# Loading the feed-forward weights of a two-layer diffusion trunk: split on chip from one copy, or by a casting and an accumulating DMA

## The chip, the cores and the metric

The kernel runs on one core of a Trainium2 chip. The metric is the device time of one execution in microseconds (us), as the median of several executions. TensorE (PE) multiplies, VectorE (DVE), ScalarE (ACT) and GpSimd (POOL) work on elements, SyncE (SP) issues DMAs; POOL can issue DMAs too.

## The reference, cut to what matters

Two layers, a mixer and a gated ConvFFN in each, over 640 tokens (512 latent, 128 context) of 1024 features, all in float32:

```
def conv_ffn(h, w_up, w_conv, w_down):
    a, g = jnp.split(h @ w_up, 2, axis=-1)
    return (jax.nn.gelu(dwconv3(a, w_conv)) * g) @ w_down
```

`w_up` has 2 x 2816 output features and `w_down` maps 2816 features back to 1024. The result must be as good as float32, so the kernel writes every operand of a large product as a sum of a high part in the reduced float32r format and a low part, the rest, and adds three products: high x high, high x low and low x high.

## The kernel before, in words

Features lie on partitions, tokens on columns. A *block* is one weight tile of 128 input rows x 8 (or 7) k-tiles x 128 outputs: 128 partitions x 1024 (or 896) float32 values, 512 KB (or 448 KB). For a block PE runs, in `mm_k` (L118), 3 products x 2 halves of 320 tokens for each k-tile: 48 matmuls, or 42 where there are 7 k-tiles. They add up in a pair of PSUM banks; there are two such pairs (L1213 and L1089: `use_psum(2, 4)`).

The feed-forward layer `ffn` (L373) has 22 feature groups f. Each takes an *up* block for `a` and one for `g`. After the `a` block, ACT and DVE convolve it out of PSUM (`conv3`, L350 and L353) and ACT takes the GELU (L388); after the `g` block, DVE multiplies (L398), and ACT and DVE split the product G into its parts (L400, L401). The *down* product runs in three passes (GROUPS, L29: k-tiles 0 to 8, 8 to 15, 15 to 22), each after the up blocks that it needs, 8 blocks a pass. So a layer has 44 up and 24 down blocks. The first three up blocks run together (`head=3`) while the norm before them is still being finished.

Weights come through `load_w` (L101): SP loads a raw block into one of 4 buffers, ACT casts it into the high part (L97), and an engine subtracts to get the low part (L98). That engine is POOL for the blocks of a head and DVE for all others. High and low parts have 3 buffers each:

```
wh = wp.tile([P, 1024], F32R, tag="wh", name=f"{nm}h")
wl = wp.tile([P, 1024], F32R, tag="wl", name=f"{nm}l")
act.copy(out=wh[:, :n], in_=raw[:, :n])
eng.tensor_tensor(out=wl[:, :n], in0=raw[:, :n], in1=wh[:, :n].bitcast(F32), op=ALU.subtract)
```

In layer 0, DVE also works on the conditioning of the other sub-layers beside the feed-forward blocks: 56 tiles `adw` of 512 KB, each loaded by SP (L244) and used by two reductions (L247).

A scheduler writes the instruction order of each engine from the program; every engine then executes its own list in order and waits at its head. A DMA waits on the issuing engine's queue, and what stands behind it waits too.

Of the kernel before, what the change touches and what calls it, by code (L numbers as in the profile page):

```python
# [10 lines left out]
F32 = mybir.dt.float32  # L11
F32R = mybir.dt.float32r
AF = mybir.ActivationFunctionType
# [3 lines left out]
P = 128  # L17
# [19 lines left out]
def trunk(ctx: ExitStack, tc: tile.TileContext, I, O, dbg=None, stop=None):  # L37
# [4 lines left out]
    wp = ctx.enter_context(tc.tile_pool(name="wp", bufs=3))  # L42
    psum = {}

    def use_psum(pairs, singles):
        """the 8 banks of PSUM: so many tiles of two banks and of one"""
        if "es" in psum:
            psum["es"].close()
        es = psum["es"] = ExitStack()
        psum["shape"] = pairs, singles  # L50
        n = psum["n"] = psum.get("n", 0) + 1
        kw = dict(space=bass.MemoryType.PSUM, reuse_waits="tile")
        psum["m"] = es.enter_context(tc.tile_pool(name=f"pm{n}", bufs=pairs, **kw))
        psum["s"] = es.enter_context(tc.tile_pool(name=f"ps{n}", bufs=singles, **kw))
# [7 lines left out]
    def bank(pt, a):  # L62
        """half a of a tile of two banks, or of two tiles of one"""
        return pt[a] if isinstance(pt, tuple) else pt[:, a]

    # ---------------------------------------------------------------- constants and persistent data
# [21 lines left out]
    # ---------------------------------------------------------------- weights: load, exact split  # L88
    def load_raw(src, nm):
        raw = wp.tile([P, 1024], F32, tag="raw", name=nm, bufs=4)  # L90
        sp.dma_start(out=raw, in_=src)
        return raw
# [7 lines left out]

    def load_w(src, nm, nk=KT, eng=dve):  # L101
        raw = wp.tile([P, 1024], F32, tag="raw", name=nm, bufs=4)
        sp.dma_start(out=raw[:, : nk * P], in_=src)
        wh, wl = split_w(raw, nk * P, nm, eng)
        return wh.rearrange("p (k c) -> p k c", c=P), wl.rearrange("p (k c) -> p k c", c=P)
# [19 lines left out]
    def linear(srcs, done, nm, ks=None, nk=KT, head=2, tail=0, by_half=True, split=SPLIT, filler=None,  # L125
               kcut=None, pre=(), hook=None, spare=False, pooled=(), x_last=False):
        """ks: (k index in the weight tile, xh, xl) in the order of arrival; head: so many first tiles run with
        k outermost; tail: so many last ones finish half by half; spare: the tile after the head in single banks;
        x_last: in the head, the low parts of the tokens come after those of the weights"""
# [4 lines left out]
        while i < n:  # L134
            left = n - i
            g = min(head, left) if i == 0 and head else (tail if tail and left == tail else 1)
            # while a norm holds the vector engine
            eng = pool if i == 0 and head and by_half or i in pooled else dve
# [40 lines left out]
    # tokens on partitions: out[tile] = X[:, tile]^T W, W 512 columns wide  # L179
# [17 lines left out]
    # ---------------------------------------------------------------- adaLN modulation  # L197
# [10 lines left out]
    # on the tensor engine, two blocks (chunk, half of it) of 512 features at once; in four steps  # L208
# [29 lines left out]
    # on the vector engine: rows of W^T times the conditioning vectors; list of steps, one per 128 features  # L238
# [17 lines left out]
    # ---------------------------------------------------------------- RMSNorm (+ adaLN), by halves of the tokens  # L256
    # (start, end, request group) of each half, and overlapping windows of 128 tokens that cover it
# [6 lines left out]
    def rms_steps(nm, a, nrm):  # L264
        """1/rms of the tokens of half a, in every partition of a PSUM tile; in two steps"""
# [18 lines left out]
        # one Newton step of 1/sqrt  # L284
# [26 lines left out]
    def norm_steps(l, which, nrm):  # L311
        """both halves, in seven steps for the end of the product before it"""
        n = 2 * l + which
        s0, s1 = (rms_steps(f"n{n}{a}", a, nrm) for a in range(2))
        next(s0)
        for _ in range(3):
            yield
        rb = next(s0)
        yield
        norm_part(l, which, nrm, 0, rb, range(0, 6))  # L320
        yield
        next(s1)
        rb1 = next(s1)
        norm_part(l, which, nrm, 0, rb, range(6, KT))
        yield
        yield norm_part(l, which, nrm, 1, rb1, range(KT))
# [8 lines left out]

    # ---------------------------------------------------------------- depthwise conv of width 3 along tokens
    # buffers: a column of padding, 512 latent tokens, padding, 128 context tokens, padding
    def halves(pt):
        """both halves of PSUM: the columns that are latent in both, and those latent in the first only"""
        return pt[:, :, 0 : NS - HT], pt[:, :, NS - HT : HT]  # L340

    def conv_parts(buf, d):
        """the same columns of a buffer, moved by d"""
        e = 1 if d > 1 else 0
        return (buf[:, 0 : 2 * HT].rearrange("p (a b) -> p a b", a=2)[:, :, d : d + NS - HT],
                buf[:, e : e + 2 * HT + 2].rearrange("p (a b) -> p a b", a=2)[:, :, NS - HT + d - e : HT + d - e])
# [9 lines left out]
    def tokens(buf):  # L356
        """(slice of the tokens, their columns of a buffer)"""
        return (slice(0, NS), buf[:, 1 : NS + 1]), (slice(P0, T), buf[:, NS + 2 : T + 2])
# [13 lines left out]
    # ---------------------------------------------------------------- ConvFFN  # L372
    def ffn(l, after, hook=None):  # L373
        with ExitStack() as es:
# [43 lines left out]
            def up(i0, i1):  # L418
                linear([I["w_up"][l, i // 2, i % 2] for i in range(i0, i1)], lambda i, pt, a: done_up(i0 + i, pt, a),
                       f"u{l}_{i0}_", head=3 if i0 == 0 else 0, filler=filler, spare=i0 == 0)  # L420

            nxt = 0
            for gi, (k0, k1) in enumerate(GROUPS):
                end = 2 * min(k1 + 1, NF)
                if end > nxt:
                    up(nxt, end)
                    nxt = end
                linear([I["w_down"][l, o, :, k0:k1] for o in range(KT)],
                       lambda o, pt, a: here.__setitem__(0, residual(l, 5, o, pt, a)), f"d{l}_{gi}_",
                       ks=[(k - k0, G[k][:, 0], G[k][:, 1]) for k in range(k0, k1)], nk=k1 - k0, head=0, filler=filler,  # L430
                       tail=3 if k1 == NF else 0, hook=hook)

    # ---------------------------------------------------------------- hyena filters (no data from x)
    def hyena_filters(fl, spectra):
        """in three parts: the loads, the filters, their spectra"""
# [18 lines left out]
        # the decay, where the first of the products with it will be  # L454
# [5 lines left out]
        for j, w in enumerate((w1, w2)):  # L460
# [18 lines left out]
            if j == 0:  # L479
                # sum and difference of the two filters' weights, twice (64 rows each), and their exact split  # L480
# [5 lines left out]
        # high parts of the hidden layer, then low parts  # L486
# [6 lines left out]
        for r in range(5):  # L493
# [8 lines left out]
            if r in (0, 4):  # L502
                # the filter of the future has no tap at 0: half of sum plus difference
# [34 lines left out]
    # ---------------------------------------------------------------- mixers A and B  # L538
    def mixer_ab():
        with ExitStack() as es:  # L540
# [9 lines left out]
            # weight tiles: (v, x1) x 4, x2 x 4, gates, q x 4, k x 4, o x 4  # L550
# [73 lines left out]
            # x holds u, then the convolved u (tiles 0-3), and x2, then y of the hyena (tiles 4-7)  # L624
            def hyena_chunk(j):
# [42 lines left out]
                # context sequence  # L668
# [64 lines left out]
            # running maxima: high parts from rows 0 and 32, low parts 64 rows further; and columns that pick both  # L733
# [7 lines left out]
            def mlstm_gates(pt, rows):  # L741
# [24 lines left out]
                # log_sigmoid(f) = min(f, 0) - log(u) + ((u - 1) - e), u = fl(1 + e)  # L766
# [79 lines left out]
            def head_a(h):  # L846
                q, k = qk[:, h], qk[:, 4 + h]
                # latent sequence
# [33 lines left out]
                # context sequence  # L882
# [19 lines left out]
            def head_b(h):  # L902
# [25 lines left out]
                # norm per head: rstd = exp(-ln(v)/2) and one Newton step  # L928
# [53 lines left out]
    # ---------------------------------------------------------------- mixer C  # L982
    # latent tokens of keys, values and queries go column by column of the grid: token c * 8 + r
    def mixer_c():
        with ExitStack() as es:
# [6 lines left out]
            # context keys of a head, the other head's rows zero  # L992
            kc = [[at.tile([P, P], F32, name=f"kc{b}{e}") for e in range(2)] for b in range(2)]
            # latent keys between 64 columns of padding, the high part twice and the low part once: with the queries
            # as (high, low) they give all products but low times low
            k1 = [[at.tile([P, 640], F32R, name=f"k1{b}{e}") for e in range(2)] for b in range(2)]
            k2 = [[at.tile([P, 640], F32R, name=f"k2{b}{e}") for e in range(2)] for b in range(2)]
            # 64 columns of padding, 512 latent tokens, 64 columns of padding, 128 context tokens
# [13 lines left out]
            # PSUM (rows 0-4 | rows 5-7, context) to column order  # L1012
# [300 lines left out]
def pack(i):  # L1313
# [10 lines left out]
    # (chunk, k pair, half, p, par, 512) and, for the other chunks, transposed (chunk, tile, p, 1024)  # L1324
# [44 lines left out]
    # rpbw[8 b + r, h, 8 a + r2]: bias of query (row r, column c) and key (row r2, column c + a - b - 8)  # L1369
# [45 lines left out]
```

## Time and profile before

| what | value |
|---|---|
| median of 3 runs | 1732.03 us (1731.26 to 1732.91) |
| profiled execution, span | 1733.2 us |
| PE busy | 1676.1 us, 97% |
| DVE busy | 1052.3 us, 61% |
| ACT busy | 672.4 us, 39% |
| POOL busy | 142.2 us, 8% |
| read from HBM | 169.61 MB |

The page gives the profiled execution by its span alone; it is 1.2 us above the median. Busy time is summed over the whole span, and the stages differ: the rows below are read by stage. The feed-forward layers lie at about 400 to 850 us and 1240 to 1710 us of the span. "Us to landing" of a DMA counts from its issue to the arrival of its last byte.

### The profile page before, as it was taken

The numbers are of one execution on the slowest core, as the hardware profiler recorded it, in microseconds if no ns is written. First come the engines' busy times: TensorE is split into PE (matmuls) and PEld (weight loads), VectorE is DVE, ScalarE is ACT, GpSimd is POOL, SyncE is SP. The second block draws the span as 40 slices with busy tenths as digits, with TensorE's granted clock in tenths as the row PEclk, the third lists the DMA queues.
The fourth block names the chain that finished last, engine by engine and source line by source line (L and its number), as shares of the span: only waits on it lengthen the run. The fifth ranks groups of instructions, "written<-read, shape, count | busy, mean of one in ns | idle before, by whom it ended". The sixth has DMA issues, their size and how long they took to land. (4 is left out here: it accounts for less than half of the span.)

```text
span 1733.2 us, 28191 instructions
## 1 busy us (share of the span) xinstructions
PE 1676.1 (97%) x11434; PEld 1596.5 (92%) x11434; DVE 1052.3 (61%) x2089; ACT 672.4 (39%) x1235; POOL 142.2 (8%) x150
## 2 busy tenths in 40 slices
PE   5999999999999999999997999999999999999997
PEld 2699889899999999999997888998999999999997
DVE  5886656666987677777376555555564433433444
ACT  6323346754432133223245565555343312321332
POOL 3110001101000000000023212120100000000001
PEclk9999999999999999999999999999999999999998
DMA  8334422141454454453213111211222222222211
GB/s 325 117 132 163 160 72 71 48 142 59 140 176 147 146 153 144 154 170 104 79 64 101 60 60 47 65 42 52 74 73 74 73 74 73 71 76 85 69 54 61
DMA packets 57121, 175.62 MB, mean 101 GB/s; under 512 B 7632, under 2 KB 15104, under 8 KB 56736
## 3 DMA queue, kind: packets, MB, share of 16 engines
q1 hardware_dynamic: 56800, 173.66, 31.1%
q8 instruction: 90, 1.47, 0.4%
q14 instruction: 39, 0.32, 0.1%
q0 software_dynamic: 192, 0.17, 0.0%
HBM read 169.61 MB, written 4.20 MB: 100 GB/s over the span
## 5 line engine op out<-in xcount | busy, mean ns | idle before, releaser
L331 DVE SCALAR_TENSOR_TENSOR x<-pd,mod,x 128x320 f32<-128x320 f32 (+2 forms) x144 | 55.1, 434 | 146.7 <-PE pd L122 137.3
L247 DVE CUSTOM_DVE_ANT_0 adj<-adw,cb 128x1024 f32<-128x1024 f32 x112 | 136.7, 1221 | 1.6
L398 DVE TENSOR_TENSOR pr<-pu,ge 128x384 f32<-128x384 f32 x84 | 37.4, 486 | 108.4 <-PE pu L122 107.6
L353 DVE SCALAR_TENSOR_TENSOR fcb<-pu,cwf,fcb 128x384 f32<-128x384 f32 (+1 forms) x176 | 95.8, 549 | 4.1
L388 ACT ACTIVATE ge<-fcb 128x641 f32<-128x641 f32 x44 | 32.6, 742 | 105.4 <-DVE fcb L353 105.4
L306 ACT ACTIVATE XH<-nt,mod 128x192 fp32r<-128x192 f32 (+1 forms) x96 | 39.6, 466 | 44.0 <-DVE nt L302 43.8
L1120 DVE CUSTOM_DVE_ANT_0 s<-pS,bm 128x384 f32<-128x384 f32 x64 | 34.5, 553 | 30.1 <-PE pS L1119 29.0
L307 DVE SCALAR_TENSOR_TENSOR XL<-nt,mod,XH 128x192 fp32r<-128x192 f32 (+1 forms) x96 | 46.4, 521 | 5.0 <-ACT XH L306 4.9
L1021 DVE TENSOR_SCALAR s<-s,nm 128x384 f32<-128x384 f32 (+1 forms) x80 | 46.3, 586 | 1.8
L1019 ACT ACTIVATE s<-s,nm 128x384 f32<-128x384 f32 x64 | 39.2, 612 | 20.3 <-DVE nm L1120 18.3
L350 ACT ACTIVATE fcb<-pu,cwf 128x384 f32<-128x384 f32 x88 | 46.3, 528 | 1.3
L1194 POOL TENSOR_TENSOR fo<-fo,rs 128x320 f32<-128x320 f32 x8 | 6.9, 888 | 469.8 <-ACT rs L1186 469.8
L1134 ACT COPY pTs<-pS 128x384 f32<-128x384 f32 (+1 forms) x80 | 33.7, 434 | 23.4 <-PE pS L1132 22.7
L1132 PE MATMUL pS<-ident,s 128*128 128x128 f32 x208 | 36.3, 281 | 5.8 <-DVE s L1021 5.8
L98 POOL TENSOR_TENSOR qk00l<-qk,qk00h 128x1024 fp32r<-128x1024 f32 x1 | 2.8, 2761 | 461.6 <-DVE rn L288 461.6
L273 ACT ACTIVATE sqn<-x 128x320 f32<-128x320 f32 x56 | 25.3, 466 | 39.4 <-DVE x L331 35.3
L1094 POOL TENSOR_TENSOR bm<-amask,wr 128x768 f32<-128x768 f32 x16 | 30.7, 1918 | 112.6 <-issue 83.9
L302 DVE SCALAR_TENSOR_TENSOR nt<-x,coefA,rbn 128x192 f32<-128x192 f32 (+1 forms) x96 | 36.7, 430 | 3.6 <-PE rbn L294 3.5
L1112 PE MATMUL pS<-k,q 128*128 128x256 f32 x128 | 31.0, 328 | 7.6 <-DVE k L1047 7.1
L400 ACT CAST G<-pr 128x640 fp32r<-128x640 f32 x44 | 31.8, 728 | 13.4 <-DVE pr L398 13.4
L331 DVE SCALAR_TENSOR_TENSOR x<-pop,mod,x 128x320 f32<-128x320 f32 (+2 forms) x36 | 14.4, 433 | 36.7 <-PE pop L122 26.0
L401 DVE TENSOR_TENSOR G<-pr,G 128x640 fp32r<-128x640 f32 x44 | 36.0, 819 | 0.0
(1110 smaller groups left out, 5507.4 us busy)
## 6 DMA issues: line engine op xcount, KB each, us to landing
u<-in_w_up SPq DMA_DIRECT2D x88, 512.0 KB, 3.5
adw<-in_w_adaT SPq DMA_DIRECT2D x56, 512.0 KB, 4.1
wa<-in_w_ada SPq DMA_DIRECT2D x40, 512.0 KB, 5.0
d<-in_w_down SPq DMA_DIRECT2D x32, 448.0 KB, 3.3
qk<-in_w_qkv SPq DMA_DIRECT2D x24, 512.0 KB, 3.5
d<-in_w_down SPq DMA_DIRECT2D x16, 512.0 KB, 3.5
qk<-in_w_ab SPq DMA_DIRECT2D x8, 512.0 KB, 3.5
op<-in_w_oab SPq DMA_DIRECT2D x6, 512.0 KB, 3.4
```

The lines of the kernel that those rows point to most:

```text
L247: dve.tensor_tensor_reduce(out=jk, in0=w, in1=cb[:, s], op0=ALU.mult, op1=ALU.add, scale=1.0, scalar=0.0, accum_out=acc[:, k, s : s + 1])
L302: dve.scalar_tensor_tensor(out=t, in0=x[:, k, c0:c1], scalar=coefA[:, n, k, s : s + 1], in1=rb[:, c0 - a * HT : c1 - a * HT], op0=ALU.mult ...
L306: act.activation(out=oh, in_=t, func=AF.Identity, bias=b)
L307: last = dve.scalar_tensor_tensor(out=ol, in0=t, scalar=b, in1=oh.bitcast(F32), op0=ALU.add, op1=ALU.subtract)
L331: r = dve.scalar_tensor_tensor(out=x[:, k, c0:c1], in0=pt[:, h, c0 - h * HT : c1 - h * HT], scalar=mod[:, l, ch, k, s : s + 1], in1=x[:, k ...
L350: act.activation(out=o, in_=i, func=AF.Copy, scale=w[1])
L353: dve.scalar_tensor_tensor(out=o, in0=i, scalar=w[j], in1=o, op0=ALU.mult, op1=ALU.add)
L398: dve.tensor_tensor(out=o, in0=i_, in1=c, op=ALU.mult)
L401: here[0] = dve.tensor_tensor(out=g[:, 1], in0=pr, in1=g[:, 0].bitcast(F32), op=ALU.subtract).ins
L1019: act.activation(out=s, in_=src, func=AF.Exp, scale=-1.0, bias=nm, accum_out=sm)
L1021: dve.tensor_scalar(out=s, in0=s, scalar1=sm, scalar2=None, op0=ALU.mult)
L1132: pe.transpose(pS[:, j * P : (j + 1) * P], s[:, j * P : (j + 1) * P], ident)
```

## The change

The feed-forward blocks that are not in the head of a layer (41 of the 44 up blocks and all 24 down blocks) are loaded by a new function. POOL issues a DMA from HBM whose destination is float32r, so that it casts: this is the high part. ACT writes its negative into the buffer of the low part. POOL issues a second DMA of the same block from HBM, which adds to that buffer: raw minus high, the low part. No raw block in SBUF, and no subtraction on DVE. High and low parts get 4 buffers each instead of 3, raw blocks 2 instead of 4 (for all other weights, too). The lines after 100 move down by 13. Comments are gone as well; the diff without them:

```
-    wp = ctx.enter_context(tc.tile_pool(name="wp", bufs=3))
+    wp = ctx.enter_context(tc.tile_pool(name="wp", bufs=4))
...
     def load_raw(src, nm):
-        raw = wp.tile([P, 1024], F32, tag="raw", name=nm, bufs=4)
+        raw = wp.tile([P, 1024], F32, tag="raw", name=nm, bufs=2)
...
+    def load_dma(src, n, nm):
+        wh = wp.tile([P, 1024], F32R, tag="wh", name=f"{nm}h")
+        wl = wp.tile([P, 1024], F32R, tag="wl", name=f"{nm}l")
+        w2 = src if len(src.shape) == 2 else src.rearrange("p k c -> p (k c)")
+        pool.dma_start(out=wh[:, :n], in_=w2)
+        act.activation(out=wl[:, :n], in_=wh[:, :n].bitcast(F32), func=AF.Copy, scale=-1.0)
+        pool.dma_start(out=wl[:, :n], in_=w2, accum_op=ALU.add)
+        return wh, wl
+
     def load_w(src, nm, nk=KT, eng=dve):
-        raw = wp.tile([P, 1024], F32, tag="raw", name=nm, bufs=4)
+        if eng is None:
+            wh, wl = load_dma(src, nk * P, nm)
+            return wh.rearrange("p (k c) -> p k c", c=P), wl.rearrange("p (k c) -> p k c", c=P)
+        raw = wp.tile([P, 1024], F32, tag="raw", name=nm, bufs=2)
...
-               kcut=None, pre=(), hook=None, spare=False, pooled=(), x_last=False):
+               kcut=None, pre=(), hook=None, spare=False, pooled=(), x_last=False, by_dma=False):
...
-            eng = pool if i == 0 and head and by_half or i in pooled else dve
+            eng = pool if i == 0 and head and by_half or i in pooled else (None if by_dma else dve)
...
-                       f"u{l}_{i0}_", head=3 if i0 == 0 else 0, filler=filler, spare=i0 == 0)
+                       f"u{l}_{i0}_", head=3 if i0 == 0 else 0, filler=filler, spare=i0 == 0, by_dma=True)
...
-                       tail=3 if k1 == NF else 0, hook=hook)
+                       tail=3 if k1 == NF else 0, hook=hook, by_dma=True)
```

The issue queue of POOL, in layer 0 in the run of up blocks (u_0_8 is up block 8; h and l are the high and the low part; in brackets what the instruction waits for). Before, POOL has no instruction here. Now:

```order
L106 DMA u_0_8h<-in_w_up 128x1024 [waits DMASW0_49,PE_49]
L108 DMA u_0_8l<-in_w_up 128x1024 [waits DMASW1_49,DMASW3_49,PE_49,Activation_49]
L106 DMA u_0_9h<-in_w_up 128x1024 [waits DMASW2_49,PE_49]
L108 DMA u_0_9l<-in_w_up 128x1024 [waits DMASW4_49,Activation_49]
L106 DMA u_0_10h<-in_w_up 128x1024 [waits PE_49]
L108 DMA u_0_10l<-in_w_up 128x1024 [waits DMASW5_49,PE_49,Activation_49]
```

The high part waits for PE, which frees a buffer; the low part waits for ACT; and the two alternate strictly, so the next block's high part stands behind this block's low part.

ACT in the same place, before (u_0_11 is cast from its raw block; fcb is the convolution of an `a` block, ge its GELU, G the product):

```order
L388 ACTIVATE ge_3_4580<-fcb_4094 128x641
L400 CAST G_3_4646<-pr_3_4643 128x640
L97 CAST u_0_11h<-u_0_11_4861 128x1024
L350 ACTIVATE fcb_4095<-pu_0_8_4662,cwf_4092 128x2x192
L350 ACTIVATE fcb_4095<-pu_0_8_4662,cwf_4092 128x2x128
L388 ACTIVATE ge_4_4717<-fcb_4095 128x641
L97 CAST u_0_12h<-u_0_12_4928 128x1024
```

and now:

```order
L401 ACTIVATE ge_3_4576<-fcb_4094 128x641
L413 CAST G_3_4641<-pr_3_4638 128x640
L107 ACTIVATE u_0_11l<-u_0_11h 128x1024
L363 ACTIVATE fcb_4095<-pu_0_8_4656,cwf_4092 128x2x192
L363 ACTIVATE fcb_4095<-pu_0_8_4656,cwf_4092 128x2x128
L107 ACTIVATE u_0_12l<-u_0_12h 128x1024
L401 ACTIVATE ge_4_4711<-fcb_4095 128x641
```

The weight's instruction keeps its place among the others, or moves ahead of one GELU; what it waits for is now a DMA that POOL has just issued, not a raw block that SP loaded blocks ahead.

ACT again, at the end of the head of layer 0, now (blocks 0, 1 and 2 are the head; up block 4's negation stands behind the convolutions of blocks 0 and 2):

```order
L363 ACTIVATE fcb_4094<-pu_0_0_4127,cwf_4092 128x2x192 [waits PE_49]
L363 ACTIVATE fcb_4094<-pu_0_0_4127,cwf_4092 128x2x128 [waits Activation_49,Pool_49]
L363 ACTIVATE fcb_4095<-pu_0_2_4129,cwf_4092 128x2x192 [waits PE_49]
L363 ACTIVATE fcb_4095<-pu_0_2_4129,cwf_4092 128x2x128 [waits Activation_49,Pool_49]
L107 ACTIVATE u_0_4l<-u_0_4h 128x1024 [waits DMASW0_49,Pool_49]
```

Before, the cast of block 4 stood between the two convolutions of block 0.

## Rows read from the trace of the kernel before

**Rows 1.** Page, head and part 1: span, busy time of each engine.
```profile
span 1733.2 us, 28191 instructions
PE 1676.1 (97%) x11434; PEld 1596.5 (92%) x11434; DVE 1052.3 (61%) x2089; ACT 672.4 (39%) x1235; POOL 142.2 (8%) x150
```
**Rows 2.** Busy us by stretch: PE, PEld, DVE, ACT, POOL; PE clock, DMA share, GB/s.
```profile
440.00:840.00 400.00, 400.00 (x2730) 400.00 (x2729) 301.09 (x496) 115.14 (x149) 0.00 (x0) 1.00 0.47 148
840.00:1240.00 400.00, 379.94 (x2786) 355.06 (x2786) 226.21 (x531) 200.88 (x457) 74.94 (x79) 0.99 0.20 63
1400.00:1500.00 100.00, 100.00 (x684) 100.00 (x683) 38.42 (x61) 25.89 (x32) 0.00 (x0) 1.00 0.24 74
```
**Rows 3.** Timeline of ACT in layer 1's up blocks: start us, us, what.
```profile
1301.38 1.05 ACT L97 CAST u_9h<-u 128x1024 fp32r<-128x1024 f32 x1 [5.03 <-PE pu L122]
1302.33 1.09 ACT L350 ACTIVATE fcb<-pu,cwf 128x384 f32<-128x384 f32 x2
1308.42 1.05 ACT L97 CAST u_10h<-u 128x1024 fp32r<-128x1024 f32 x1 [1.68 <-PE pu L122]
1315.46 1.05 ACT L97 CAST u_11h<-u 128x1024 fp32r<-128x1024 f32 x1 [5.03 <-PE pu L122]
1519.61 0.94 ACT L97 CAST d_0h<-d 128x896 fp32r<-128x896 f32 x1 [1.68 <-PE pu L122]
```
**Rows 4.** Timeline of DVE, same place.
```profile
1302.45 1.22 DVE L98 TENSOR_TENSOR u_9l<-u,u_9h 128x1024 fp32r<-128x1024 f32 x1 [5.00 <-ACT u_9h L97]
1303.60 2.31 DVE L353 SCALAR_TENSOR_TENSOR fcb<-pu,cwf,fcb 128x384 f32<-128x384 f32 x4
```
**Rows 5.** DMA issues: what, queue, count, KB each, median us to landing.
```profile
u<-in_w_up SPq DMA_DIRECT2D x88, 512.0 KB, 3.5
d<-in_w_down SPq DMA_DIRECT2D x32, 448.0 KB, 3.3
d<-in_w_down SPq DMA_DIRECT2D x16, 512.0 KB, 3.5
```
**Rows 6.** Timeline of POOL at the program's start: its DMA issues.
```profile
1.98 0.54 POOL L1211 DMA_DIRECT2D selc<-in_k_selc  x1
2.51 0.53 POOL L1211 DMA_DIRECT2D gains<-in_gains  x1
```
**Rows 7.** DMA issues, small ones, all but cwf in the first 5 us.
```profile
ident<-in_k_ident POOLq DMA_DIRECT2D x1, 64.0 KB, 3.5
bada<-in_b_ada POOLq DMA_DIRECT2D x1, 48.0 KB, 2.9
fw<-in_w_f SPq DMA_DIRECT2D x2, 32.0 KB, 3.3
fb<-in_f_cols SPq DMA_DIRECT2D x1, 1.0 KB, 3.1
cond<-in_cond SPq DMA_DIRECT2D x1, 8.0 KB, 1.6
cwf<-in_w_conv_ffn SPq DMA_DIRECT2D x2, 33.0 KB, 1.7
```
**Rows 8.** Timeline of ACT at the end of layer 0's head.
```profile
439.39 1.05 ACT L97 CAST u_3h<-u 128x1024 fp32r<-128x1024 f32 x1 [1.19 <-PE pu L116]
440.35 0.58 ACT L350 ACTIVATE fcb<-pu,cwf 128x384 f32<-128x384 f32 x1
```
**Rows 9.** DMA issues from 500 to 820 us, beside the adw loads.
```profile
adw<-in_w_adaT SPq DMA_DIRECT2D x43, 512.0 KB, 4.3
u<-in_w_up SPq DMA_DIRECT2D x27, 512.0 KB, 3.6
```
**Rows 10.** Busy us by stretch, as in Rows 2: the two heads.
```profile
370.00:440.00 70.00, 67.04 (x456) 65.83 (x455) 45.09 (x105) 30.02 (x54) 7.50 (x3) 1.00 0.24 77
1230.00:1290.00 60.00, 57.48 (x393) 56.49 (x392) 44.88 (x101) 29.99 (x55) 7.51 (x3) 1.00 0.19 63
```
**Rows 11.** Who waited for whom on PE: us in total, times, longest.
```profile
PE pu L116 <- DVE XL L307: 2.0, 2, 1.0
```

## The prediction

> **What bounds the kernel now.** I read the page first, then the stages by busy time per stretch, then the timelines of ACT, DVE and POOL, and last the DMA issues. By the page PE is busy 97% of the span [rows 1]. The stages say where: inside a feed-forward layer PE has no gap at all, 100.00 us busy of 100 with 684 matmuls, at a granted clock of 1.00, its upper level of 2.4 GHz [rows 2]. DVE stands at 75% there in layer 0 and at 38% in layer 1, ACT under 30%, the DMA engines at 0.47 and 0.24, POOL at 0.00 [rows 2]. So nothing that the change takes from DVE or SP ends a wait of PE there. On the timeline an ACT instruction that is released by the end of an up block comes back after two blocks: 1301.38 and 1315.46 us, 14.08 us apart [rows 3], so a block of 48 matmuls takes **7.04 us**, and one of 42 matmuls 7.04 x 42 / 48 = **6.16 us**. That is the time in which weights must come: 98 of the blocks that change have 48 matmuls (2 x 41 up, 16 down), 32 have 42 (the 448 KB loads), as the counts of the loads say, 88 + 48 less 6 in the heads [rows 5].
>
> **What goes.** 130 subtractions on DVE of 1.22 us [rows 4], some 155 us of busy time, and 130 loads on SP. The cover is PE: it is at 100%, so this is worth nothing inside a layer. SP loses work that nobody waits for.
>
> **What stays.** ACT's cast of 1.05 us (0.94 for 448 KB) [rows 3] becomes a negation of the same size, taken at the same price. Its wait is new: it holds ACT until a DMA lands. Behind it in ACT's list is the convolution of an `a` block, and behind that DVE and the PSUM pair. ACT's and DVE's shares of a convolution take 1.09 + 2.31 us [rows 3, 4], and the pair is wanted only a whole block later, 7.04 us, so some 3.6 us of lateness costs nothing. As long as the loads keep pace, the DMA lands about 2 us before that `a` block ends, and ACT is not late.
>
> **What is added: a chain on POOL.** POOL was idle here, and the order alternates strictly: cast of block i, accumulate of block i, cast of block i + 1. The accumulate waits for the negation, which waits for the cast to land. So two casts are apart by at least the cast's landing, the negation and the issue of the accumulate, however many buffers there are. The links of this period, each with its bounds:
>
> - Landing of the cast, 512 KB. SP's plain load takes 3.5 us [rows 5]. POOL's only loads are small: 48 and 64 KB land in 2.9 and 3.5 us; SP's small ones take 3.1 and 3.3 us in the same crowded first microseconds, but 1.6 and 1.7 us without the crowd [rows 7]. So POOL's path adds between 0 and 3.5 - 1.6 = 1.9 us: 3.5 to 5.4 us. I take 4.4, the middle, since either row is as near.
> - Queueing behind the accumulate of the block before, which POOL issued 0.53 us earlier [rows 6]. A plain 512 KB load occupies the 16 engines for 524288 B / 74 GB/s x 0.24 = 1.7 us [rows 2]; the cast then waits 1.7 - 0.53 = 1.2 us. Bounds: 0, if they overlap; 2 x 1.7 - 0.53 = 2.9 us, if an accumulate takes the engines twice as long because it also reads its target. I take 1.2, the plain row.
> - Negation 1.05 us [rows 3], two semaphore hops of about 0.1 us, issue of the accumulate 0.53 us [rows 6]: 1.8 us.
>
> The period is 4.4 + 1.2 + 1.8 = **7.4 us**, with ends 5.3 and 10.1 us. For 448 KB: 0.2 us less to land [rows 5], 0.2 less queueing, 0.1 less on ACT [rows 3]: 6.9 us. Both are over PE's block, so the chain sets the pace.
>
> The Trainium skill (DMA: Bandwidth & Descriptors, "Anatomy of one DMA — SWDGE (gpsimd) path") gives about 2.0 us plus bytes / 436 GB/s for a DMA from GpSimd, an estimate of 3.2 us for this block; no large POOL load in the trace tests it. By it the period would be 6.2 us and the second rival below would come true.
>
> **The sum,** against the span of 1733.2 us:
>
> - 98 blocks x (7.4 - 7.04) = +35 us.
> - 32 blocks x (6.9 - 6.16) = +24 us.
> - Layer 0: 56 `adw` loads share the engines. Beside them u's loads take 3.6 instead of 3.5 us, and adw itself 4.3 [rows 5, 9]: between 0.1 and 0.8 us per load. The chain waits for every load of its own, so I take 0.8: +45 us (lower end +6).
> - Slack: with 4 buffers a cast can go out 3 blocks (21.1 us) before its block starts, and needs 7.4 + 4.4 us: PE feels the lag only after some 9 us in each layer, -18 us.
> - Heads: up block 4's cast must wait for block 0's buffer, free at 439.4 us [rows 8], and its negation now stands behind the convolutions of blocks 0 and 2, which ends about 443 us; accumulate landed about 450 us, when block 3 ends too. 0 to 2 us per layer; +2 us in all.
> - Raw buffers 2 instead of 4 elsewhere: a load of 3.5 us [rows 5] against blocks of 7 us; two are enough. 0, with up to 3 us either way from an order that shifts a little.
> - Clock: PE's gaps would be some 5%. The stretch between the layers has 5% gaps and a clock of 0.99 [rows 2]: 0.
> - HBM: about 66 MB more, DMA share 0.47 + 0.24 = 0.7 in layer 0, 0.5 in layer 1. Not a bound if an accumulate costs what a copy costs.
>
> Together +88 us: 1821 us, and 1.2 us less against the median: **1820 us**. POOL's own split of the head blocks stays ahead of the first cast in its queue, and SP's next loads no longer stand behind feed-forward loads; neither is on the path.
>
> **The rivals.**
>
> - *The accumulate is dear.* It takes the DMA engines twice as long (queueing 2.9 us). Period 9.1 and 8.4 us: 98 x 2.06 + 32 x 2.24 + 45 - 18 + 2 = +303, 2035 us; with the landing at 5.4 us too, 10.1 us, some 2160 us. For it: the target must be read and added to, and in layer 0 the engines would come to 0.47 + 0.47. Against it: no row shows such a DMA. Chance 0.14. The Trainium skill (DMA: Bandwidth & Descriptors, "Rules for kernel authors") says that an accumulate reads its destination and writes it later, which speaks for this rival.
> - *The chain fits.* Landing 3.5 us and little queueing: period 5.3 to about 6.4 us, under or at PE's block; PE stays at 100% and only the heads lose 0 to 2 us each: 1732 to 1737 us, 1734 at the middle. For it: SP's and POOL's small loads are alike in the same crowd [rows 7]. Against it: it needs both unknown links near their lower ends. Chance 0.27 (0.20 within 0.2%, 0.06 above, 0.01 below).
> - *Faster: the heads profit.* Point of decision: period at or below 6.2 us, and the accumulate of block 4 in time. Then DVE, which in the heads is the engine that PE waits for (the last part of the norm, 2.0 us [rows 11]), has the subtractions of blocks 3 to 6 off its list, and PE may win back what it lacks there: 70 - 67.04 and 60 - 57.48, 5.5 us together [rows 10]: 1727 us. Against it: those subtractions mostly stand behind the norm, not in it. Chance 0.09.
>
> **How the numbers follow.** A measurement of this kernel can tell about 0.2%, 3.5 us, from no change. My forecast, the chain over PE's block with a period of some 6.5 to 8.8 us, has 0.50, and all of it is slower; with the dear accumulate 0.14 and 0.06 of the second rival: slower 0.70, same 0.20, faster 0.09 + 0.01 = 0.10. The upper end: a period of 8.8 us gives 98 x 1.76 + 32 x 2.1 + 29 = +268, 2000 us; above it lies mainly the first rival. The lower end, 1728, takes in the second rival and leaves out most of the third.
>
> **What would show it.** Right: PE in the feed-forward layers at some 93 to 96% instead of 100%, its matmuls waiting for the accumulating DMA; casts on POOL spaced 7 to 8 us, the wait in front of the accumulate ended by ACT, and ACT's by the cast's landing; the `conv3` of ACT late. Down blocks of 448 KB lose most per block, layer 0 more than layer 1. Wrong: PE still at 100.00 there (the chain fits), casts that land under 4 us, or casts that take 7 us and more alone (then the first rival's size). Also wrong in its reason would be time lost outside these layers, by raw buffers.

## The result, and the profile after

The changed kernel takes **1960.16 us** (median of 4 runs, 1956.3 to 1962.1), the kernel before 1732.47 us beside it: a ratio of 1.131, 95% interval 1.129 to 1.132. It is 228 us slower. The profiled execution spans 1958.2 us, 225.0 more than before.

The page of the changed kernel, head, part 1 and the row of POOL's DMA queue (packets, MB, share of the 16 engines over the span):

```profile
span 1958.2 us, 28257 instructions
PE 1736.5 (89%) x11434; PEld 1630.2 (83%) x11434; DVE 915.4 (47%) x1959; ACT 668.4 (34%) x1235; POOL 326.7 (17%) x410
q0 software_dynamic: 37632, 132.31, 30.4%
```

Against [rows 1], DVE has the 130 subtractions less and some 137 us of busy time less, POOL 260 DMA issues more, and PE is at 89% instead of 97%. Busy us by stretch, to be read beside [rows 2] (columns as there; the last stretch has no counterpart there, and before, PE was busy 100.00 us of it too):

```profile
440.00:840.00 400.00, 337.09 (x2128) 328.17 (x2126) 193.12 (x354) 84.67 (x110) 64.79 (x91) 0.95 0.71 177
1400.00:1500.00 100.00, 93.86 (x632) 92.28 (x631) 26.51 (x49) 31.14 (x42) 19.12 (x27) 1.00 0.59 132
1500.00:1600.00 100.00, 87.34 (x568) 84.46 (x567) 17.63 (x39) 17.37 (x21) 16.10 (x23) 0.98 0.57 126
```

PE executes 568 matmuls in 100 us where it had 684. The stretch from 1400 us still lives on the blocks loaded ahead; the next one doesn't. The first and the last matmul of the feed-forward in each layer (up block 0 and down block 7), on PE's timeline before and after:

```profile
416.94 0.31 PE L113 MATMUL pu<-XH,u_0h 128*128 128x320 f32 x1
...
886.40 0.31 PE L116 MATMUL pd<-G,d_7l 128*128 128x320 f32 x1
...
1248.90 0.31 PE L113 MATMUL pu<-XH,u_0h 128*128 128x320 f32 x1
...
1717.34 0.31 PE L116 MATMUL pd<-G,d_7l 128*128 128x320 f32 x1
```

```profile
418.09 0.31 PE L126 MATMUL pu<-XH,u_0h 128*128 128x320 f32 x1
...
1019.18 0.31 PE L129 MATMUL pd<-G,d_7l 128*128 128x320 f32 x1
...
1379.94 0.31 PE L126 MATMUL pu<-XH,u_0h 128*128 128x320 f32 x1
...
1940.82 0.31 PE L129 MATMUL pd<-G,d_7l 128*128 128x320 f32 x1
```

Up to layer 0's feed-forward the change costs 1.2 us. Layer 0's feed-forward takes 601.4 us instead of 469.8, layer 1's 561.2 instead of 468.8: +131.6 and +92.4 us, 224 of the 225. What lies between and behind them makes up less than 1 us. (From the start of one feed-forward to the start of the next it is 961.9 us instead of 832.0, and from there to the end 578.3 instead of 484.3: +130 and +94 us.)

Now the chain on POOL. Its timeline in layer 1 (start us, us, what, in brackets the idle time ahead and what ended it), and ACT's for the same blocks:

```profile
1574.71 0.85 POOL L108 DMA_DIRECT2D d_7l<-in_w_down  x1 [7.21 <-ACT d_7l L107]
1575.25 0.87 POOL L106 DMA_DIRECT2D u_0h<-in_w_up  x1
1582.98 0.87 POOL L108 DMA_DIRECT2D u_0l<-in_w_up  x1 [6.85 <-ACT u_0l L107]
1583.52 0.89 POOL L106 DMA_DIRECT2D u_1h<-in_w_up  x1
```

```profile
1581.62 1.06 ACT L107 ACTIVATE u_0l<-u_0h 128x1024 fp32r<-128x1024 f32 x1 [7.21 <-DMA u_0h<-in_w_up]
1590.00 1.06 ACT L107 ACTIVATE u_1l<-u_1h 128x1024 fp32r<-128x1024 f32 x1 [7.32 <-DMA u_1h<-in_w_up]
```

One period can be read off link by link: the cast goes out at 1575.25, ACT starts 6.37 us later, when it has landed, and takes 1.06; 0.30 us after that POOL issues the accumulate, and 0.54 us later, at 1583.52, the next cast. That is 8.27 us, against 7.04 us that PE needs for the block. POOL's waits end with ACT, ACT's with the DMA: nothing else is in the loop.

The landings say where the 6.37 us come from. DMA issues, first where the head ends and u_4h has nothing ahead of it on POOL's queue, then in the running chain in layer 1, from 1400 to 1700 us (KB, median us to landing):

```profile
u_4h<-in_w_up POOLq DMA_DIRECT2D x1, 512.0 KB, 3.9
```

```profile
u_10h<-in_w_up POOLq DMA_DIRECT2D x2, 512.0 KB, 6.2
u_10l<-in_w_up POOLq DMA_DIRECT2D x2, 512.0 KB, 6.0
u_12l<-in_w_up POOLq DMA_DIRECT2D x2, 512.0 KB, 5.6
```

So 3.9 us are the cast's own (4.0 for the same block in layer 1) and 2.3 us are spent behind the accumulate of the block before. The DMA engines' busy share (tenths) and rate from 1560 to 1605 us, in slices of 1.1 us, show the same in each period: a slow part (the accumulate), a fast part (the cast), then a gap in which ACT negates and POOL issues:

```profile
DMA  9991005699900077996001999900088993007899
GB/s 193 208 386 55 0 0 36 87 208 244 335 22 0 0 58 131 211 313 233 0 0 18 127 175 244 350 18 0 0 91 138 211 379 113 0 0 62 120 200 302
```

The packets in the trace show it too. POOL's queue moved some 3070 packets of 4096 bytes between 1500 and 1600 us; about half of them took 174 ns (median) and the other half 328 ns, and in the period read above nearly all the slow ones come before the first fast one.

The engines are far from full over time (0.57 from 1500 to 1600 us). They are in the way for just as long as they hold up the next link.

### The profile page after: what moved, and what is told of

Read it like the earlier page. It is cut to its first block, busy times and chain, and to the rows that moved or that the text cites. A ratio compares the mean times of both kernels' runs of the same rounds, so it can differ in the third digit from the quotient of the medians.

```text
span 1958.2 us, 28257 instructions
## 1 busy us (share of the span) xinstructions
PE 1736.5 (89%) x11434; PEld 1630.2 (83%) x11434; DVE 915.4 (47%) x1959; ACT 668.4 (34%) x1235; POOL 326.7 (17%) x410
## 5 line engine op out<-in xcount | busy, mean ns | idle before, releaser
L135 PE MATMUL pd<-G,d_0h 128*128 128x320 f32 x176 | 35.0, 320 | 14.9 <-ACT G L413 14.9
L287 DVE TENSOR_TENSOR accn<-accn,sqn 128x320 f32<-128x320 f32 x56 | 35.0, 630 | 24.7 <-ACT sqn L286 23.7
L320 DVE SCALAR_TENSOR_TENSOR XL<-nt,mod,XH 128x192 fp32r<-128x192 f32 (+1 forms) x96 | 40.8, 462 | 5.5 <-ACT XH L319 5.5
L135 PEld LDWEIGHTS pd<-G,d_0h 128*128 128x128 f32 x176 | 28.4, 194 | 16.1 <-ACT G L413 15.4
L135 PE MATMUL pd<-G,d_4h 128*128 128x320 f32 x176 | 36.0, 330 | 0.0
```

The source lines that it names most:

```text
L135: pe.matmul(bank(pt, a)[:, : sp_[a][1] - sp_[a][0]], ww[:, kt], xx[:, slice(*sp_[a])], start=(first and n == 0), stop=(last and n == 2))
L320: last = dve.scalar_tensor_tensor(out=ol, in0=t, scalar=b, in1=oh.bitcast(F32), op0=ALU.add, op1=ALU.subtract)
```

## Experiments

**The theory** after the result: the loop cast, negation, accumulate, next cast sets the pace, since POOL issues the next cast only behind an accumulate that has itself waited; and it is longer than forecast since an accumulate occupies the engines longer than a plain load. **Rivals:** the DMA engines or HBM can't carry a cast and an accumulate per block at PE's pace; or the `adw` loads, or the number of buffers, make the difference.

**1. The next block's cast ahead of this block's accumulate.** The same DMAs, the same negation and the same bytes; POOL's order differs, except for the first block of a layer. By the traces ACT's list moves too, but only by a place or two at the head of a layer.

```
+    def cast():
...
+        st.append((wh, wl, w2, n, pool.dma_start(out=wh[:, :n], in_=w2)))
...
+        cast()
+        wh, wl, w2, n, _ = st.pop(0)
         act.activation(out=wl[:, :n], in_=wh[:, :n].bitcast(F32), func=AF.Copy, scale=-1.0)
+        with tc.issue_after(st[-1][4].ins) if st and n0[0] > 1 else ExitStack():
             pool.dma_start(out=wl[:, :n], in_=w2, accum_op=ALU.add)
```

> Chain theory (the pace is set by cast, landing, negation and accumulate following each other on POOL's queue): with the next block's cast issued ahead of this block's accumulate the chain spans two blocks, some 4.2 us per block, and the DMA engines need about 1.3 us (cast) + 3.6 us (accumulate) of 7.04 us. PE goes back to about 100% in the feed-forward layers; 1732 to 1742 us. Rival (the DMA engines cannot carry the accumulates at PE's pace, whatever the order): time stays at 1930 us or more, with PE still waiting for the accumulates.

Measured: 1733.98 us (1732.7 to 1735.2), ratio to the kernel before 1.0003, interval 0.9994 to 1.0013. Busy us by stretch, and POOL's timeline:

```profile
520.00:840.00 320.00, 320.00 (x2184) 320.00 (x2183) 181.66 (x334) 85.33 (x108) 66.31 (x92) 1.00 0.90 217
1400.00:1500.00 100.00, 100.00 (x684) 100.00 (x683) 23.55 (x47) 25.59 (x32) 20.22 (x28) 1.00 0.72 151
```

```profile
1488.98 0.55 POOL L110 DMA_DIRECT2D u_29h<-in_w_up  x1 [5.61 <-PE pu L148]
1489.52 0.92 POOL L120 DMA_DIRECT2D u_28l<-in_w_up  x1
1496.03 0.55 POOL L110 DMA_DIRECT2D u_30h<-in_w_up  x1 [5.58 <-PE pu L148]
1496.56 0.91 POOL L120 DMA_DIRECT2D u_29l<-in_w_up  x1
```

PE is back at 684 matmuls per 100 us, the casts are 7.05 us apart, and what ends POOL's wait is now PE, which frees a buffer, not ACT. The DMA engines are at 0.90 in layer 0 and PE has no gap there. The whole 226 us hung on the order of POOL's queue; the rival with the engines or HBM as the bound falls.

**2. A second DMA that copies instead of adding.** The order of the changed kernel, with the accumulate made a copy, so that the low part holds the whole weight.

```
-        pool.dma_start(out=wl[:, :n], in_=w2, accum_op=ALU.add)
+        pool.dma_start(out=wl[:, :n], in_=w2)
```

> The second DMA copies (and casts) instead of adding; all waits and the order stay, so the low part is wrong (the whole weight). Theory that the mis-sized term is the accumulate's engine time, 3.6 instead of 1.7 us, before which the next cast queues: the cast's landing falls from 6.2 to about 4.7 us, the period to 6.7 us, and the time to 1740 to 1765 us. Rival (POOL's path or the cast itself is slow): the cast's landing stays over 6 us and the time over 1930 us.

Measured: 1767.6 us (one run), a little above what was expected and 193 us under the changed kernel. Busy us by stretch, POOL's timeline in layer 0, and two landings in layer 1:

```profile
440.00:840.00 400.00, 379.87 (x2534) 374.46 (x2534) 223.75 (x411) 101.82 (x132) 56.99 (x109) 0.99 0.64 209
1400.00:1500.00 100.00, 100.00 (x684) 100.00 (x683) 20.84 (x45) 22.23 (x27) 14.78 (x28) 1.00 0.48 148
```

```profile
627.50 0.54 POOL L106 DMA_DIRECT2D u_4h<-in_w_up  x1
633.49 0.53 POOL L108 DMA_DIRECT2D u_4l<-in_w_up  x1 [5.45 <-ACT u_4l L107]
634.01 0.54 POOL L106 DMA_DIRECT2D u_5h<-in_w_up  x1
639.93 0.53 POOL L108 DMA_DIRECT2D u_5l<-in_w_up  x1 [5.38 <-ACT u_5l L107]
640.45 0.54 POOL L106 DMA_DIRECT2D u_6h<-in_w_up  x1
```

```profile
u_10h<-in_w_up POOLq DMA_DIRECT2D x1, 512.0 KB, 4.6
u_10l<-in_w_up POOLq DMA_DIRECT2D x1, 512.0 KB, 3.7
```

With a copy the cast lands in 4.6 us instead of 6.2, and an undisturbed period is 6.4 us (634.01 to 640.45), under PE's block. In layer 1 PE is at 100%. What is left is lost in layer 0, where casts are 7.24 us apart in the mean, the head's three quick ones included; the `adw` loads lie there, but this wasn't tried without them. So the same chain, with a second DMA that takes the engines no longer than the first, would have all but fitted: the adding is what the forecast had too cheap.

**What an accumulate takes from the engines** can also be had from four kernels. The row of POOL's queue from 1500 to 1600 us, in layer 1, where hardly anything else is on the engines: packets, MB, share of the 16 engines, which is also the us in this stretch of 100. In order: plain loads on POOL (experiment 6), cast and copy (experiment 2), cast and accumulate with the cast ahead (experiment 1), and the changed kernel.

```profile
q0 software_dynamic: 1785, 7.47, 24.3%
```

```profile
q0 software_dynamic: 4050, 13.76, 45.5%
```

```profile
q0 software_dynamic: 4387, 14.96, 72.7%
```

```profile
q0 software_dynamic: 3444, 12.54, 56.3%
```

Per 0.524 MB that is 24.3 x 0.524 / 7.47 = 1.70 us for a plain load and 1.73 for a casting DMA: the cast costs the engines nothing that these rows show. The mean of a cast and an accumulate is 2.55 us in experiment 1 and 2.35 in the changed kernel, so, if a cast still takes 1.73 beside it, an accumulate takes 2 x 2.55 - 1.73 = **3.4 us** and 2 x 2.35 - 1.73 = **3.0 us**, 1.7 to 2.0 times a plain load; the packets, 328 against 174 ns, say 1.9. The Trainium skill (DMA: Bandwidth & Descriptors, "Rules for kernel authors") says that an accumulate reads its destination and writes it later; the rows, at nearly twice a plain load, agree with a second pass over the data.

**3. No `adw` loads.** 55 of layer 0's 56 loads of 512 KB are gone.

```
-            w = pl.tile([P, 1024], F32, tag="adw", name=f"adw{l}{ch}{k}", bufs=2)
-            sp.dma_start(out=w, in_=I["w_adaT"][6 * l + ch - 5, k])
+            if "adw" not in psum:
+                w = psum["adw"] = pl.tile([P, 1024], F32, tag="adw", name="adw", bufs=1)
+                sp.dma_start(out=w, in_=I["w_adaT"][6 * l + ch - 5, k])
+            w = psum["adw"]
```

> The changed kernel without 55 of the 56 adw loads of layer 0 (one tile is used for all, so the conditioning values are wrong). Theory that the adw loads share the DMA engines and lengthen the chain: layer 0 loses the same 94 us as layer 1 instead of 130 us, 1958 - 36 = 1922 us. Rival (layer 0 loses more because DVE is busier there): no change, 1958 us.

Measured: 1904.37 us (one run); its span is 55.6 us shorter than that of the changed kernel, more than the 36 expected. Busy us in layer 0:

```profile
440.00:840.00 400.00, 355.23 (x2349) 344.35 (x2348) 208.03 (x383) 92.99 (x120) 71.67 (x101) 1.00 0.56 128
```

PE has 2349 matmuls there instead of 2128, still far from the 2730 of [rows 2]. Layer 0's feed-forward takes 552.2 us, 49 less than in the changed kernel and now no more than layer 1's; most of the rest of the 55.6 us lies in layer 1 and is taken up under what was not expected. So the `adw` loads, and not a busier DVE, which still has its work here, make layer 0's extra loss: contention with `adw` is a part of layer 0's loss, not the cause of the whole.

**4. The buffer counts alone.** The kernel before with 4 high and 4 low parts and 2 raw blocks.

```
-    wp = ctx.enter_context(tc.tile_pool(name="wp", bufs=3))
+    wp = ctx.enter_context(tc.tile_pool(name="wp", bufs=4))
...
-        raw = wp.tile([P, 1024], F32, tag="raw", name=nm, bufs=4)
+        raw = wp.tile([P, 1024], F32, tag="raw", name=nm, bufs=2)
```

> The kernel before with only the change of buffers (raw 2 instead of 4, high and low parts 4 instead of 3). Prediction: no cost, 1729 to 1736 us. Rival (some of the loss is from fewer raw buffers): 1745 us or more.

Measured: 1729.53 us (1728.2 to 1731.6), ratio 0.9976, interval 0.9965 to 0.9987. It is the one part of the change that helps, by 0.2%. Busy us in the two heads, first of this kernel, then with the cast ahead (experiment 1):

```profile
440.00:520.00 80.00, 80.00 (x547) 80.00 (x546) 71.24 (x119) 29.50 (x38) 0.00 (x0) 1.00 0.55 175
1240.00:1290.00 50.00, 50.00 (x345) 49.82 (x344) 39.25 (x89) 26.35 (x47) 1.92 (x1) 1.00 0.25 81
```

```profile
440.00:520.00 80.00, 78.37 (x534) 78.10 (x533) 55.02 (x99) 28.95 (x38) 17.61 (x24) 1.00 0.97 244
1240.00:1290.00 50.00, 47.63 (x326) 46.93 (x326) 33.29 (x85) 23.95 (x44) 11.40 (x13) 1.00 0.48 110
```

With the cast ahead PE lacks 1.6 and 2.4 us there, about the 4.5 us between the two kernels.

**5. The cast ahead, from up block 8 on.** Against experiment 1:

```
-            eng = pool if i == 0 and head and by_half or i in pooled else (by_dma or dve)
+            eng = pool if i == 0 and head and by_half or i in pooled else (by_dma if by_dma and (not head or i >= 8) else dve)
...
-                order += [(I["w_up"][l, i // 2, i % 2], 1024, f"u{l}_{i}") for i in range(max(nxt, 3), end)]
+                order += [(I["w_up"][l, i // 2, i % 2], 1024, f"u{l}_{i}") for i in range(max(nxt, 8), end)]
```

> As the experiment with the next block's cast ahead, but in each layer only from up block 8 on; blocks 3 to 7 are loaded raw by SP and split by ACT and DVE as before, with the changed buffer counts. The buffers alone gave 1729.5 us, the cast ahead 1734.0, and its two layers' heads (440 to 520 and 1240 to 1290 us) show 1.6 and 2.4 us of PE lost. Head theory: what the cast ahead lacks against the buffers alone is the first chain link at the end of the head, so this lands at 1729 to 1731. Rival (the DMA engines at 0.9 in layer 0, or the two loads of each block, cost PE a little everywhere): 1733 to 1735, as before. The third rival of the prediction (DVE's relief makes the heads faster) would show as under 1727.

Measured: 1729.55 us (1727.7 to 1732.3), ratio to the kernel before 0.9979, interval 0.9970 to 0.9988. That is the time of the buffers alone, with 120 blocks loaded by two DMAs each: the head's first link was all that experiment 1 lacked. With the heads left out of it the two DMAs cost nothing, and DVE's 120 subtractions fewer bring nothing. Nothing in this study is faster than its simplest version, the kernel before with the buffers of the change.

**6. Plain raw loads on POOL.** The kernel before, with its feed-forward loads on POOL's queue.

```
-        sp.dma_start(out=raw[:, : nk * P], in_=src)
+        (pool if nm[0] in "ud" else sp).dma_start(out=raw[:, : nk * P], in_=src)
```

> The kernel before, with the raw feed-forward blocks loaded by POOL instead of SP, no cast, no accumulate. Measures one disputed link: the landing of a plain 512 KB load from POOL's queue. The forecast took 4.4 us for the cast (bounds 3.5 to 5.4); the changed kernel's casts land in 3.9 us where nothing is ahead of them. If the cast itself costs nothing, this load lands in 3.7 to 4.0 us; if the cast costs, in 3.5. Time 1731 to 1737 us, since loads are issued blocks ahead.

Measured: 1730.92 us (one run), just under the range expected. DMA issues of this kernel:

```profile
u<-in_w_up POOLq DMA_DIRECT2D x88, 512.0 KB, 3.8
```

POOL's path adds 0.3 us to the 3.5 of [rows 5], not 0.9, and the cast some 0.1. The Trainium skill (DMA: Bandwidth & Descriptors, "Anatomy of one DMA — SWDGE (gpsimd) path") gives 2.0 us plus bytes / 436 GB/s, an estimate of 3.2 us; the measured 3.8 decides.

**7. The changed kernel with the buffers of before** (3 high, 3 low, 4 raw).

```
-    wp = ctx.enter_context(tc.tile_pool(name="wp", bufs=4))
+    wp = ctx.enter_context(tc.tile_pool(name="wp", bufs=3))
...
-        raw = wp.tile([P, 1024], F32, tag="raw", name=nm, bufs=2)
+        raw = wp.tile([P, 1024], F32, tag="raw", name=nm, bufs=4)
```

> The changed kernel with the buffer counts of the kernel before: 3 high and 3 low parts, 4 raw blocks. Chain theory: the period on POOL is landing + negation + accumulate's issue and does not depend on the number of buffers, so the casts stay 8.2 us apart in layer 1; only the lead before PE feels the lag shrinks by one block of 7 us in each layer, of which the heads may give some back: 1960 to 1975 us. Rival (buffers come free too late and set the pace): period 9 us or more, over 2000 us.

Measured: 1977.1 us (one run), 2 us beyond the range that the chain theory gave. POOL's timeline in layer 1:

```profile
1598.60 0.89 POOL L106 DMA_DIRECT2D u_0h<-in_w_up  x1
1606.21 0.87 POOL L108 DMA_DIRECT2D u_0l<-in_w_up  x1 [6.72 <-ACT u_0l L107]
1606.75 0.89 POOL L106 DMA_DIRECT2D u_1h<-in_w_up  x1
```

The period is 8.15 us here and 8.21 in the median over layer 1, as with four buffers. A buffer buys a lead, once per layer; it doesn't change the pace. The rival with the buffers falls.

## Why the prediction was right in its mechanism and short in its size

The forecast named the loop on POOL, and it is what sets the pace: PE falls from 100% to 84 to 87% in the feed-forward and waits for the accumulates, casts are 8.2 us apart (layer 1's median; 8.7 in layer 0's mean), POOL's wait is ended by ACT and ACT's by the landing. Experiment 1 shows it, by taking the loop apart and nothing else. The range, 1728 to 2000 us, holds the result. But the forecast was +88 us, and it is +228.

**The term that failed is the queueing of the cast behind the accumulate**: "1.2 us, the plain row". It measured 2.3 us (6.2 - 3.9). What it had wrong is the price of an accumulate on the engines, taken as that of a plain load, 1.7 us: it is 3.0 to 3.4. So the end "2 x 1.7 - 0.53 = 2.9 us, if an accumulate takes the engines twice as long because it also reads its target" was the nearer one. Experiment 2 parts the two: behind a copy the cast lands 0.7 us late (4.6 - 3.9), and behind an accumulate 1.6 us later still. The rule itself, engine time less 0.53 us, asks for too much: 1.2 us behind a copy, and 2.5 to 2.9 behind an accumulate. The mechanism of the first rival was the true one, at a chance of 0.14; its 2035 us came out too long since its landing, 4.4 us, is 0.5 too long and its queueing, 2.9 us, 0.6.

Term by term, with what the runs showed:

- Landing of the cast alone: 3.9 us, forecast 4.4. Taking the middle of two bounds was 0.5 us too much, and hid a part of the queueing's error by luck. "Casts that land under 4 us" was named as a sign against the forecast; it came true for this one cast, and in the chain they take 6.2.
- Negation, hops and issue: 1.06 + 0.30 + 0.54, with some 0.1 us from landing to ACT: 2.0 us, forecast 1.8.
- Period: 3.9 + 2.3 + 2.0 = 8.2 us, forecast 7.4. The error of 0.8 us is small beside a period, and large beside 7.4 - 7.04 = 0.36, the quantity that is multiplied by 98: it comes to 98 x 1.16 = +114 us, forecast +35.
- 448 KB: 7.8 us between casts in layer 1's second run of down blocks (1700.91 to 1724.28 us, three periods): 32 x 1.64 = +52 us, forecast +24.
- `adw` in layer 0: 49 us in experiment 3, forecast 45 (it had 6 as the lower end).
- Slack: forecast -18 us, and the kernel's end gives most of it back. The last three down blocks are done together, half by half, so that after the last accumulate PE still has 13 us of work instead of 6. PE's timeline, the first matmul that uses the last low part, 13 us before the feed-forward ends at 1941 us:

```profile
1928.16 0.42 PE L129 MATMUL pd<-G,d_7l 128*128 128x320 f32 x1 [3.08 <-DMA d_7l<-in_w_down]
```

That leaves -18 + 2 x (13 - 6.2) = about -4 us, an estimate from this row.

- Heads: 4.4 us in all between experiments 1 and 5, forecast 2.
- Buffer counts: forecast 0 for the raw blocks, with up to 3 us either way; the counts alone gave -3.6 us (1729.53 against 1733.15 us beside it).
- Clock: the granted clock fell to 0.95 in layer 0. A block of 7.04 us would take 7.4 us there, still less than the mean period of 8.7 us, so 0 stands, argued and not tried alone.
- HBM and the engines: no bound, as forecast. Experiment 1 runs them at 0.90 of the time with PE at 100%.

The sum with the measured terms is 114 + 52 + 49 - 4 + 4 - 4 = +211, against +225 in the span. The rest, 14 us, is of the size of the long periods, below, which the medians leave out; it was not traced further.

The same can be had from one subtraction: from the cast of up block 4 to that of the last down block layer 1 takes 514.6 us, and with the cast ahead, where PE sets the pace, 422.1 us. POOL's timeline of the changed kernel, then of experiment 1:

```profile
1401.16 0.55 POOL L106 DMA_DIRECT2D u_4h<-in_w_up  x1 [14.62 <-PE pu L129]
...
1915.75 0.88 POOL L106 DMA_DIRECT2D d_7h<-in_w_down  x1
```

```profile
1267.51 0.56 POOL L110 DMA_DIRECT2D u_4h<-in_w_up  x1 [14.63 <-PE pu L142]
...
1689.62 0.55 POOL L110 DMA_DIRECT2D d_7h<-in_w_down  x1 [4.71 <-PE pd L148]
```

The difference, 92.5 us, is the 92.4 us that layer 1's feed-forward lost.

The second rival (the chain fits) fell with the accumulate's price; experiment 2 shows how near it was, since with a copy it holds in layer 1. The third (the heads profit from DVE's relief) fell too: in experiment 5 DVE has 120 subtractions less, and the time is that of the buffers alone.

## What to carry to other kernels

Where DMAs and engines alternate on one in-order queue, write the loop down and compare its length with the consumer's pace; only the difference counts, so an uncertain link of 1 us can be worth ten times its share of the sum, and the bounds of the period should be multiplied out before a middle is taken. A loop like this one is broken by issuing the next block's first step ahead of this block's last, which here gave back 226 us with the same transfers. By these runs, with blocks of 512 KB, an accumulating DMA is to be priced at nearly two plain ones on the engines, and a casting one as a plain one.

## What was not expected

- A casting DMA from POOL costs the engines no more than a plain load (1.73 and 1.70 us), and lands some 0.1 us later (3.9 and 3.8 us).
- Now and then, in layer 1 about every eighth block, a period is 9 to 10 us. In one of these (down block 4, at 1732.96 us) POOL issues the accumulate 1.6 us after ACT is done, instead of 0.3, with no wait that the profile shows. The same block shows it most in experiment 2: there ACT's negation of d_4 ends at 1577.08 us, and POOL's next DMA starts at 1579.94, 2.9 us later. The cause of the long periods stays open.

POOL's timeline in experiment 2:

```profile
1579.94 0.53 POOL L108 DMA_DIRECT2D d_4l<-in_w_down  x1 [7.76 <-issue]
```

- Without the `adw` loads layer 1 became 5 us shorter too (555.8 instead of 561.2 us from its first to its last feed-forward matmul), though none lie there; not explained.
- POOL is busy 0.85 to 0.92 us with an accumulate, and with a cast right behind one, against 0.53 to 0.56 us for other DMA issues. The next instruction starts after 0.54 us all the same, so on POOL this had no part in the period.
